# Gram matrices ahead of the values, side steps that may be put off, and a start that turns x a quarter at a time

## The chip, the cores and the metric

One core of a Trainium2 chip runs the whole program. Its engines are TensorE (PE, with a weight-load path PEld beside it), VectorE (DVE), ScalarE (ACT), GpSimd (POOL) and SyncE (SP, which here only issues DMAs). The time is the device time of one execution in microseconds; the median of three runs stands for a kernel, and one further run was profiled.

## The reference, cut to what matters

The layer normalizes x (256 x 2048), multiplies it by one large matrix (2048 x 20672) and feeds three branches: A is block attention over 12 heads of 128, B a recurrence (RWKV7) over 24 heads of 64, C attention to a memory over 4 heads of 256. The three are gated, projected, summed, multiplied by w_out and added to x.

```python
h = rms_norm(x, norm_g)
proj = h @ w_in                       # 2048 x 20672
qkv_a, z_a, rkv_b, z_b, lw, la, q_c, z_c, gates = split(proj)
y_a = moba_attention(q_a, k_a, v_a, rel_bias) * silu(z_a)
# branch B: per head a 64x64 state, one step per token
sa    = state @ a_t
state = state * w_t + outer(sa, b_t) + outer(v_t, k_t)
y_t   = state @ r_t
y_b = (groupnorm(y) * lnx_w + lnx_b + bonus) * silu(z_b)
y_c = memory_cross_attention(q_c, mem_n @ w_mem_kv) * silu(z_c)
merged = g_a*(y_a @ w_proj_a) + g_b*(y_b @ w_proj_b) + g_c*(y_c @ w_proj_c)
out = rms_norm(x + merged @ w_out, final_norm_g)
```

The kernel does branch B in chunks of 128 tokens: for each head a Gram matrix of the chunk's vectors, the solution of a triangular system, and a few products with it.

## The kernel before, in words

**The main stream.** All weights come from HBM in chunks of 512 KB (384 KB for the first job, the LoRA inputs lw and la) into a `raw` buffer (three of them; SP issues the DMA). ACT copies a chunk's high half into a `wt` buffer (L270), DVE writes what is left as the low half (L273) and so frees `raw` for the next DMA. PE multiplies the split weights by the split, transposed x (`hT`): L308 with 512 columns needs the high half only, L309 with 256 columns the low half; "wide" jobs use L306. Sums go into four PSUM banks `pm`. A chunk of a job is a round: `prefetch` starts DMAs and splits up to three chunks ahead (in the first four rounds only the chunk of the round itself), `issue_mm` issues the products for two halves f = 0 and 1, and `step_lanes` then runs one step of each side lane. A round of 16 products takes PE about 2.8 us.

**The side lanes** are generators; what one step issues lands on the engines' queues behind that round's products. Each engine works its queue in order, so a side matmul that waits holds up the next round's main products. Side matmuls share four other PSUM banks, `psd`. `pairs_lane(g)`, for the six groups g of four heads of branch B, computes the decays, the scaled r and k (`AR`, `BK`), then in one step, after V has come, turns two products to sum them per head (L590, L591), turns V and part of BK (L599 to L601) and starts `rw_lane(g)`: the Gram matrices of two token chunks c = 0 and 1 on PE (L622), which DVE scales and masks into `GS` (L626, L627), one step each. Blocks of GS go through DRAM (SP, L652 out and L663 back as `NB`), DVE solves the triangular systems (L674, L678), and further products follow. `attn_a(g)` is branch A's attention: scores, softmax, transposed probabilities, product with v. `later` starts a small lane such as `spread_rows`, whose DMA `fr<-fd` (L421, on ACT's queue) copies a row of the attention's bias to 128 rows.

**The start.** `x_stats` sums squares of x, keeps PE busy with transposes of an identity, and splits the first chunk with its low half held back. `x_quarter(q)` scales 512 columns of both token halves (ACT one, DVE the other, L916 and L917) and transposes them (L154); its `fin` moves the transposes into `hT` as a high half (ACT, L159) and a low half (DVE, L162). Round 0 of the LoRA job does quarters 0 and 1; rounds 1 and 2 begin with quarters 2 and 3. At round 3 the parameter rows and the bias table are turned (L118, L413), the bias is sent to DRAM from ACT's queue (L415), and behind that ACT takes the next job's splits.

## Time and profile before

| | us |
| --- | --- |
| runs | 1479.2, 1479.53, 1478.37 |
| median | 1479.2 |
| profiled execution, own time | 1478.29 |
| its span | 1476.5 |
| outside the span | 1.8 |
| PE busy | 1449.2 |
| DVE busy | 946.2 |
| ACT busy | 747.3 |

The profiled execution is 0.9 us below the median, so a difference worked out in its span is carried to the median as it is. PE is the engine to read: what it waits for, and where.

### The profile page before, as it was taken

How to read it: one execution, taken by the hardware profiler on the slowest of the kernel's cores; microseconds unless marked ns; L12 is line 12 of the kernel's file. 1: busy time of each engine (PE TensorE's matmuls, PEld its weight loads, DVE VectorE, ACT ScalarE, POOL GpSimd, SP SyncE). 2: the span in 40 equal slices, each digit the busy share in tenths (PEclk: the TensorE clock that was granted, in tenths of full speed). 3: DMA queues.
4: the chain of work that ended last, by engine and by line, in shares of the span. 5: the costliest groups of instructions: out<-in, count | busy, mean ns of one | idle time of the engine just before them, and what ended most of it. 6: DMA issues, size and time to landing. Idle time of an engine off the chain costs nothing.

```text
span 1476.5 us, 22151 instructions
## 1 busy us (share of the span) xinstructions
PE 1449.2 (98%) x8315; PEld 1222.3 (83%) x8315; DVE 946.2 (64%) x1855; ACT 747.3 (51%) x1122; POOL 181.8 (12%) x252
## 2 busy tenths in 40 slices
PE   7999999999999999999999999999999999999997
PEld 6887888888888788788888888888888888888887
DVE  5778697796795786784666555655545545545555
ACT  5546546466456456445666454643443444444443
POOL 4312202212212222211100000000000000000011
PEclk9999999999999999999999999999999999999999
DMA  5665555456465465465575555566556556555753
GB/s 180 192 179 163 159 147 169 143 167 173 133 184 151 134 172 159 135 178 158 162 221 187 172 169 174 167 196 192 187 188 195 188 187 194 188 188 192 262 200 130
DMA packets 207968, 258.88 MB, mean 175 GB/s; under 512 B 28172, under 2 KB 146596, under 8 KB 207220
## 3 DMA queue, kind: packets, MB, share of 16 engines
q1 hardware_dynamic: 201872, 247.11, 54.5%
q10 hardware_dynamic: 4164, 6.71, 1.3%
q0 software_dynamic: 1824, 3.65, 0.8%
q8 instruction: 65, 1.06, 0.3%
q14 instruction: 43, 0.35, 0.1%
HBM read 253.74 MB, written 6.05 MB: 176 GB/s over the span
## 4 chain that ended last, share of the span: by engine, by line
PE 89%; DVE 4%; DMA 2%; ACT 1%; issue 1%; POOL 1%; SPq 0%; ACTq 0%; DVEq 0%
PE pm L306 43%; PE pm L308 24%; PE pm L309 12%; PE psd L622 2%; DVE wt L273 1%; DMA raw<-in_w_in_dram 1%; DVE fs_t L674 1%; PE psd L641 1%; PE psd L1037 1%; PE psd L743 1%; DMA NB<-d 1%; PE psd L154 1%; DMA x_sb<-in_x_dram 1%; ACT wt L270 1%; DVE X L678 1%
## 5 line engine op out<-in xcount | busy, mean ns | idle before, releaser
L273 DVE TENSOR_TENSOR wt<-raw,wt 128x1024 fp32r<-128x1024 f32 (+1 forms) x451 | 559.1, 1242 | 437.4 <-ACT wt L270 433.8
L270 ACT ACTIVATE wt<-raw 128x1024 fp32r<-128x1024 f32 (+1 forms) x452 | 477.2, 1057 | 494.0 <-PE pm L306 256.5
L308 PE MATMUL pm<-hT,wt 128*128 128x512 f32 (+1 forms) x1632 | 587.1, 402 | 0.0
L309 PE MATMUL pm<-hT,wt 128*128 128x256 f32 (+1 forms) x1632 | 458.5, 281 | 3.5 <-DVE wt L273 3.4
L308 PEld LDWEIGHTS pm<-hT,wt 128*128 128x128 f32 (+1 forms) x1632 | 305.7, 187 | 76.3 <-issue 4.2
L306 PE MATMUL pm<-wt,hT 128*128 128x512 f32 x1440 | 335.4, 391 | 0.0
L306 PEld LDWEIGHTS pm<-wt,hT 128*128 128x128 f32 x1440 | 268.6, 188 | 57.6 <-issue 1.7
L309 PEld LDWEIGHTS pm<-hT,wt 128*128 128x128 f32 (+1 forms) x1632 | 307.5, 188 | 6.2 <-DVE wt L273 6.0
L306 PE MATMUL pm<-wt,mg 128*128 128x512 f32 (+1 forms) x384 | 79.3, 367 | 0.0
L306 PEld LDWEIGHTS pm<-wt,mg 128*128 128x128 f32 x384 | 65.7, 189 | 12.5
L1183 POOL MEMSET sso<- 128x16 f32 x1 | 0.1, 117 | 607.0 <-PE pm L306 607.0
L674 DVE TENSOR_TENSOR fs_t<-X,NB 128x30 f32<-128x30 f32 (+13 forms) x354 | 64.9, 223 | 7.5 <-DMA NB<-d 7.1
L306 PE MATMUL pm<-wt,yas 128*128 128x512 f32 x288 | 67.6, 395 | 0.0
L306 PE MATMUL pm<-wt,ybs 128*128 128x512 f32 x288 | 67.6, 395 | 0.0
L323 POOL TENSOR_TENSOR lraw<-lraw,et 128x256 f32<-128x256 f32 (+1 forms) x38 | 45.1, 1207 | 167.2 <-ACT lraw L322 167.2
L306 PEld LDWEIGHTS pm<-wt,ybs 128*128 128x128 f32 x288 | 54.3, 188 | 12.6
L306 PEld LDWEIGHTS pm<-wt,yas 128*128 128x128 f32 x288 | 54.3, 188 | 12.7
L317 ACT ACTIVATE et<-pm 128x256 f32<-128x256 f32 (+1 forms) x112 | 42.6, 382 | 40.3 <-PE pm L309 37.6
L678 DVE TENSOR_TENSOR X<-X,fs_t 128x30 f32<-128x30 f32 (+13 forms) x354 | 56.3, 194 | 0.6
L306 PE MATMUL pm<-wt,mT 128*128 128x512 f32 x192 | 45.8, 395 | 0.0
L308 PE MATMUL pm<-mT,wt 128*128 128x512 f32 x128 | 45.4, 395 | 0.0
L306 PE MATMUL pm<-wt,ycs 128*128 128x512 f32 x192 | 45.3, 395 | 0.0
(299 smaller groups left out, 1324.3 us busy)
## 6 DMA issues: line engine op xcount, KB each, us to landing
raw<-in_w_in_dram SPq DMA_DIRECT2D x320, 512.0 KB, 3.7
raw<-in_w_mem_kv_dram SPq DMA_DIRECT2D x32, 512.0 KB, 3.5
raw<-in_w_out_dram SPq DMA_DIRECT2D x32, 512.0 KB, 4.4
raw<-in_w_proj_a_dram SPq DMA_DIRECT2D x24, 512.0 KB, 4.2
raw<-in_w_proj_b_dram SPq DMA_DIRECT2D x24, 512.0 KB
raw<-in_w_proj_c_dram SPq DMA_DIRECT2D x16, 512.0 KB, 4.4
NB<-d SPq DMA_DIRECT2D x24, 128.0 KB, 3.4
fr<-fd ACTq DMA_DIRECT2D x6, 385.0 KB
```

What stands on the lines that cost most here:

```text
L154: pe.transpose(pv[:, a, t], src[:, t, (k + a) * 128:(k + a + 1) * 128], ident)
L270: act.activation(w[:, :, 0], r, AF.Copy)
L273: eng.tensor_tensor(w[:, :, 1], r, w[:, :, 0].bitcast(FT), OP.subtract)
L306: pe.matmul(ps[:, 0:j.n], l, r, start=first and n == 0, stop=last and n == 2)
L308: pe.matmul(ps[0:j.m], hi, both, start=first, stop=last, skip_group_check=True)
L309: pe.matmul(ps[0:j.m, 256:512], lo, top, start=False, stop=last, skip_group_check=True)
L317: act.activation(t, ps[0:j.m, 256:512], AF.Copy)
L323: pool.tensor_tensor(j.dst[f], j.dst[f], t, OP.add)
L622: pe.matmul(pv[h][:, w].rearrange("p x t -> p (x t)"), BK[rows, q, c, w * 128:(w + 1) * 128], AR[rows, q, c].rearrange("p x t -> p (x t)") ...
L641: pe.matmul(pv[:, 2 * q + h], GS[:, c * 4 + 2 * q + h, 2], tok[:, q, c, rows], start=(c == 0), stop=True, skip_group_check=True)
L674: dve.tensor_tensor(t, X[:, k0:8, c:c + 1].to_broadcast([128, m, hi - lo]), NB[:, lo:hi, c].rearrange("p (o n) -> p o n", o=1).to_broadcas ...
L678: dve.tensor_tensor(X[:, k0:8, lo:hi], X[:, k0:8, lo:hi], t, OP.add)
```

## The change

Four edits. (1) `step_lanes` knows a yield (d, more): after d rounds the step may be put off for up to `more` rounds, until a round in which another lane took a `psd` bank; it stands ahead of the decay products (from g = 1 on), the values, the attention's scores, its transposed probabilities and its product with v. (2) In `pairs_lane` the two summed products no longer wait for V; `rw_lane` is started right behind them, two rounds later it issues the Gram matrices, and the turning of V and BK is a later step of its own. Two waits on `rkv_free` are added, one before the next group's BK is written and one before the solved blocks are copied. (3) `x_quarter` becomes `x_scale` and `x_turn`: before round 0 one quarter is turned (each pair of its transposes in a bank of its own) and another scaled on DVE alone; then, in the middle of rounds 0 to 2 between the two halves f, the next quarter is turned, the one behind it scaled and the turned one moved to `hT`. (4) The first chunk's low half goes to POOL at once in place of DVE later, and the identity transposes before the first real ones are 20 in place of 18.

```diff
@@ -145,21 +148,22 @@
         dve.scalar_tensor_tensor(r, s, 1.5, r, op0=OP.add, op1=OP.mult)
         return r
-    def turned(src, g_nm, dst, k):
-        p = ps_side()
-        pv = p.rearrange("p (a t c) -> p a t c", a=2, t=2)
+    def turned(src, g_nm, dst, k, apart=False):
+        banks = [ps_side()]
+        banks.append(ps_side() if apart else banks[0])
+        pv = [two(p)[:, a] for a, p in enumerate(banks)]
         for a in range(2):
             for t in range(2):
-                pe.transpose(pv[:, a, t], src[:, t, (k + a) * 128:(k + a + 1) * 128], ident)
+                pe.transpose(pv[a][:, t * 128:t * 128 + 128], src[:, t, (k + a) * 128:(k + a + 1) * 128], ident)
         def fin():
             for a in range(2):
                 g = pcol(g_nm, k + a)
-                act.activation(dst[:, k + a, 0], two(p)[:, a], AF.Copy, scale=g)
+                act.activation(dst[:, k + a, 0], pv[a], AF.Copy, scale=g)
             for a in range(2):
                 g = pcol(g_nm, k + a)
-                dve.scalar_tensor_tensor(dst[:, k + a, 1], two(p)[:, a], g, dst[:, k + a, 0].bitcast(FT),
+                dve.scalar_tensor_tensor(dst[:, k + a, 1], pv[a], g, dst[:, k + a, 0].bitcast(FT),
                                          op0=OP.mult, op1=OP.subtract)
         return fin
...
@@ -207,16 +213,26 @@
             yield 1
         add_lane(g(), rest)
+    def step(ln):
+        try:
+            d = next(ln[1])
+            d, more = d if isinstance(d, tuple) else (d or 1, 0)
+            ln[0], ln[2] = clock[0] + d, more
+        except StopIteration:
+            lanes.remove(ln)
     def step_lanes():
         clock[0] += 1
-        for ln in list(lanes):
-            if ln[0] > clock[0]:
-                continue
-            try:
-                d = next(ln[1])
-                ln[0] = clock[0] + (d or 1)
-            except StopIteration:
-                lanes.remove(ln)
+        n = used[0]
+        due = [ln for ln in lanes if ln[0] <= clock[0]]
+        for ln in due:
+            if not ln[2]:
+                step(ln)
+        for ln in due:
+            if ln[2] and ln[0] <= clock[0]:
+                if used[0] != n or clock[0] >= ln[0] + ln[2]:
+                    ln[2] = 0
+                    step(ln)
     def force(*keys):
         n = 0
...
@@ -355,6 +371,8 @@
             if c == 0:
                 j.ps[f] = ps_main()
             products(j, j.ps[f], f, c, w)
+            if f == 0 and j.mid:
+                j.mid(c)
             if end:
                 if j.mode == "wide":
                     j.evac(j.ps[f], f)
...
@@ -514,7 +532,7 @@
         wa = rw.tile([96, 256], FT, name="wa")
         pool.dma_start(wd, w_decay2[0][:, c0:c0 + 256])
         pool.dma_start(wa, w_aaa2[0][:, c0:c0 + 256])
-        yield 3
+        yield (3, 2) if g else 3
         p = ps_side()
         sg = rw.tile([128, 2, 256], FT, name="sg")
         for q in range(2):
...
@@ -572,15 +590,13 @@
         dve.tensor_tensor(AR[:, :, :, 0], c2(kk), ep[:, :, :, 0:128], OP.mult)
         dve.scalar_tensor_tensor(av, av, 1.0, kk, op0=OP.add, op1=OP.mult)
         if g:
-            yield from wait(("gram", g - 1))
+            yield from wait(("gram", g - 1), ("rkv_free", g - 1))
         yield 1
         BK = rw.tile([128, 2, 2, 256], FT, name="BK")
         dve.tensor_tensor(BK[:, :, :, 0:128], c2(av), en[:, :, :, 1:129], OP.mult)
         dve.tensor_tensor(BK[:, :, :, 128:256], c2(km), en[:, :, :, 1:129], OP.mult)
         dve.tensor_tensor(esc, ep[:, :, 0, 128], en[:, :, 1, 0], OP.mult)
         flags["decay_free", g] = True
-        yield 1
-        yield from wait(("V", g))
         yield 1
         for t, o in ((sq, nb), (r, bs)):
             p = ps_side()
...
@@ -591,6 +607,10 @@
             dve.tensor_reduce(o.rearrange("p c q h -> p (c q h)"), p.rearrange("p (u v) -> p u v", u=8), AX.X, OP.add)
         dve.tensor_scalar(nb, nb, 1e-24, -2.0, op0=OP.max, op1=OP.mult)
         dve.reciprocal(nb, nb)
+        add_lane(rw_lane(g, AR, BK, tok, nb, bs, esc), 2)
+        yield 1
+        yield from wait(("V", g))
+        yield (1, 2)
         v = St.pop(("V", g))
         for q in range(2):
             p = ps_side()
...
@@ -604,7 +624,6 @@
                 dve.tensor_scalar(tok[:, q, 3, 64 * h:64 * h + 64], pv[:, 3, 64 * h:64 * h + 64],
                                   nb[:, 0, q, h:h + 1], None, op0=OP.mult)
         flags["rkv_free", g] = True
-        add_lane(rw_lane(g, AR, BK, tok, nb, bs, esc))
         yield 1
     def rw_lane(g, AR, BK, tok, nb, bs, esc):
...
@@ -687,6 +706,7 @@
             nc.sync.dma_start(XN[s], d2[8 * d:8 * d + 8].rearrange("u k r c -> (k r) u c"))
         yield 3
         dve.transpose(XT, XN)
+        yield from wait(("rkv_free", g))
         yield 1
         for s in D4:
...
@@ -832,6 +852,7 @@
         yield from wait(("qa", g), ("ka", g))
         if g:
             yield from wait(("soft", g - 1))
+        yield (1, 2)
         q, k = St[("qa", g)], St[("ka", g)]
         p1_, p0_ = ps_side(), ps_side()
         for h in range(2):
...
@@ -868,8 +889,8 @@
                 pe.transpose(p[:, i * 128:i * 128 + 128], s[:, h, o:o + 128], ident)
             act.activation(pT[:, h], p[:, 0:384], AF.Copy)
         flags["soft", g] = True
-        yield 1
         yield from wait(("va", g))
+        yield (1, 2)
         v = St[("va", g)]
         p = ps_side()
         for h in range(2):
...
@@ -898,36 +917,39 @@
                                      accum_out=sp[:, 1, h:h + 1])
             issue_dma(nc.scalar)
         p = ps_side()
-        pe.transpose(p[:, 0:128], x_sb[:, 0, 0:128], ident)
-        for i in range(18):
-            if i == 11:
+        for h in range(2):
+            pe.transpose(p[:, 0:128], x_sb[:, 0, h * D // 2:h * D // 2 + 128], ident)
+            for i in range(10):
+                pe.transpose(p[:, 0:128], ident, ident)
+            if h == 0:
                 turn_params(prow1, "1", 16)
-            pe.transpose(p[:, 0:128], ident, ident)
         ss = stat.tile([128, 2], FT, name="x_ss")
         dve.tensor_reduce(ss, sp, AX.X, OP.add)
         v, s = rsqrt_a(ss, 2, 1.0 / D, 0, "n")
         issue_dma(nc.scalar)
-        issue_split(hold=held)
+        issue_split(pool)
         norm_r.append(rsqrt_b(v, s, 2, "n"))
-    def x_quarter(q):
+    def x_scale(q, first=act):
         r, cs = norm_r[0], slice(512 * q, 512 * q + 512)
-        act.activation(x_sb[:, 0, cs], x_sb[:, 0, cs], AF.Copy, scale=r[:, 0:1])
+        if first is act:
+            act.activation(x_sb[:, 0, cs], x_sb[:, 0, cs], AF.Copy, scale=r[:, 0:1])
+        else:
+            dve.tensor_scalar(x_sb[:, 0, cs], x_sb[:, 0, cs], r[:, 0:1], None, op0=OP.mult)
         dve.tensor_scalar(x_sb[:, 1, cs], x_sb[:, 1, cs], r[:, 1:2], None, op0=OP.mult)
-        fins[q] = [turned(x_sb, "g", hT, 4 * q + 2 * a) for a in range(2)]
+    def x_turn(q):
+        return [turned(x_sb, "g", hT, 4 * q + 2 * a, apart=(q == 0)) for a in range(2)]
     def lora_pre(c):
         if c == 0:
             x_stats()
-            x_quarter(0)
-            x_quarter(1)
-            held.pop()()
-        elif c < 3:
-            x_quarter(c + 1)
-        for f in fins.pop(c):
-            f()
-        if c == 0:
+            x_scale(0)
+            fins = x_turn(0)
+            x_scale(1, dve)
+            for f in fins:
+                f()
             issue_split(pool)
             consts.append(consts_lane())
             next(consts[0])
...
@@ -935,7 +957,16 @@
             next(consts[0])
             prefetch(3, 6)
-    jobs = [Job(w_in2, LW, 192, 16, hT, lora_evac, m=96, pre=lora_pre, add=pool)]
+    def lora_mid(c):
+        if c < 3:
+            fins = x_turn(c + 1)
+            if c < 2:
+                x_scale(c + 2)
+            for f in fins:
+                f()
+    jobs = [Job(w_in2, LW, 192, 16, hT, lora_evac, m=96, pre=lora_pre, mid=lora_mid, add=pool)]
     RJ, AJ = [], []
     for g in range(NG):
         c = g * 256
```

On PE, in the mains around group g = 1 of branch B, the side work of that group stood like this before (L780 turns the output of the group ahead, L590 the two summed products, L599 to L601 V and BK of one of two head pairs, L622 is the Gram of chunk c; L306 are main products):

```order
L306 MATMUL pm<-wt,hT 128x512 x24
L780 MATMUL psd<-ident,YT 128x128 x4
L590 MATMUL psd<-ident,sg 128x128 x4
L590 MATMUL psd<-ident,R 128x128 x4
L599 MATMUL psd<-ident,V 128x128 x2
L600 MATMUL psd<-ident,BK 128x128
L601 MATMUL psd<-ident,BK 128x128
...
L306 MATMUL pm<-wt,hT 128x512 x12
L622 MATMUL psd<-AR,BK 128x256 x8
```

The same place in the changed kernel (L800 is the old L780, L606 the old L590, L619 to L621 the old L599 to L601, L641 the old L622, L322 the old L306):

```order
L606 MATMUL psd<-ident,sg 128x128 x4
L606 MATMUL psd<-ident,R 128x128 x4
L322 MATMUL pm<-wt,hT 128x512 x12
L800 MATMUL psd<-ident,YT 128x128 x4
L322 MATMUL pm<-wt,hT 128x512 x12
L641 MATMUL psd<-AR,BK 128x256 x8
L619 MATMUL psd<-ident,V 128x128 x2
L620 MATMUL psd<-ident,BK 128x128
L621 MATMUL psd<-ident,BK 128x128
...
L322 MATMUL pm<-wt,hT 128x512 x12
L641 MATMUL psd<-AR,BK 128x256 x8
```

One interruption with 20 transposes has become two, of eight and of four, each a round apart; the eight that turn V and BK now follow the Gram of c = 0 in its interruption. The number of interruptions is the same.

On SP's queue, from the program's first weight load to the triangular system of g = 0 (`d` is the block of GS in DRAM), before:

```order
L259 DMA raw<-in_w_in_dram 128x4x192
L259 DMA raw<-in_w_in_dram 128x4x256 x24
L652 DMA d_951<-GS 32x8x32 x4
L259 DMA raw<-in_w_in_dram 128x4x256
L663 DMA NB<-d_951 32x1024 x4
```

And changed:

```order
L275 DMA raw<-in_w_in_dram 128x4x192
L275 DMA raw<-in_w_in_dram 128x4x256 x23
L671 DMA d_933<-GS 32x8x32 x4
L275 DMA raw<-in_w_in_dram 128x4x256
L682 DMA NB<-d_933 32x1024 x4
```

The Gram's way through DRAM starts one weight load, that is one round, earlier.

On ACT, from the first split to the DMA that takes the bias to DRAM, before (L270 is a split's high half, L916 a scaling of x, L159 four high halves of `hT`):

```order
L270 ACTIVATE wt<-raw 128x4x192
L916 ACTIVATE x_sb<-x_sb,rs_rn 128x512 x2
L159 ACTIVATE hT<-psd,par_138 128x256 x4
L270 ACTIVATE wt<-raw 128x4x192
L916 ACTIVATE x_sb<-x_sb,rs_rn 128x512
L159 ACTIVATE hT<-psd,par_138 128x256 x4
L270 ACTIVATE wt<-raw 128x4x192
L916 ACTIVATE x_sb<-x_sb,rs_rn 128x512
L159 ACTIVATE hT<-psd,par_138 128x256 x4
L270 ACTIVATE wt<-raw 128x4x192
L159 ACTIVATE hT<-psd,par_138 128x256 x4
L415 DMA fd<-fb 12x385
```

And changed (L286, L937 and L163 in their places):

```order
L286 ACTIVATE wt<-raw 128x4x192
L937 ACTIVATE x_sb<-x_sb,rs_rn 128x512
L163 ACTIVATE hT<-psd,par_137 128x256 x4
L286 ACTIVATE wt<-raw 128x4x192
L937 ACTIVATE x_sb<-x_sb,rs_rn 128x512
L163 ACTIVATE hT<-psd,par_137 128x256 x4
L937 ACTIVATE x_sb<-x_sb,rs_rn 128x512
L163 ACTIVATE hT<-psd,par_137 128x256 x4
L286 ACTIVATE wt<-raw 128x4x192
L163 ACTIVATE hT<-psd,par_137 128x256 x4
L286 ACTIVATE wt<-raw 128x4x192
L433 DMA fd<-fb 12x385
```

The third and the fourth split have changed places with the four high halves of `hT` ahead of which they stood; one scaling has gone to DVE.

## Rows read from the trace of the kernel before

**Rows 1.** Waits of PE, then of PEld: us in total, times, longest.
```profile
PE psd L599 <- DVE Y L790: 3.4, 5, 0.9
PE psd L622 <- DVE GS L627: 2.3, 4, 0.6
PE psd L700 <- ACT pT L869: 0.4, 1, 0.4
...
PEld pm L309 <- DVE wt L273: 6.0, 8, 1.2
```
**Rows 2.** Timeline of the start: start, us, engine, line, operation [idle before <- releaser].
```profile
12.41 0.88 DVE L917 TENSOR_SCALAR x_sb<-x_sb,rs_rn 128x512 f32<-128x512 f32 x2
...
13.24 3.54 PE L154 MATMUL psd<-ident,x_sb 128*128 128x128 f32 x16 [3.03 <-ACT x_sb L916]
...
16.54 0.47 PE L308 MATMUL pm<-hT,wt 128*96 128x512 f32 x1
...
16.91 1.85 POOL L273 TENSOR_TENSOR wt<-raw,wt 128x768 fp32r<-128x768 f32 x1 [5.30 <-ACT wt L270]
16.92 2.12 DVE L917 TENSOR_SCALAR x_sb<-x_sb,rs_rn 128x512 f32<-128x512 f32 x1
...
19.43 1.03 PE L154 MATMUL psd<-ident,x_sb 128*128 128x128 f32 x8
...
20.11 1.59 ACT L159 ACTIVATE hT<-psd,par 128x256 fp32r<-128x256 f32 x4
...
21.53 0.90 ACT L270 ACTIVATE wt<-raw 128x768 fp32r<-128x768 f32 x1
...
23.38 0.94 DVE L273 TENSOR_TENSOR wt<-raw,wt 128x768 fp32r<-128x768 f32 x1
...
27.08 0.29 DVE L120 COPY par<-psd 128x128 f32<-128x128 f32 x1 [0.82 <-PE psd L118]
...
31.20 0.39 PE L309 MATMUL pm<-hT,wt 128*128 128x256 f32 x1 [0.44 <-DVE wt L273]
```
**Rows 3.** Timeline, PE and DVE, group g = 1: values, then the first Gram.
```profile
181.61 0.60 PE L780 MATMUL psd<-ident,YT 128*128 128x128 f32 x4
...
184.40 2.98 PE L306 MATMUL pm<-wt,hT 128*128 128x512 f32 x12
187.31 2.00 PE L622 MATMUL psd<-AR,BK 64*128 64x256 f32 x16
188.48 0.48 DVE L626 SCALAR_TENSOR_TENSOR GS<-psd,nb,msk 128x256 f32<-128x256 f32 x1 [1.00 <-PE psd L622]
...
189.21 0.47 DVE L626 SCALAR_TENSOR_TENSOR GS<-psd,nb,msk 128x256 f32<-128x256 f32 x1
189.24 0.98 PE L306 MATMUL pm<-wt,hT 128*128 128x512 f32 x3
```
**Rows 4.** Timeline, PE, group g = 4: values, then the first Gram.
```profile
492.74 0.60 PE L780 MATMUL psd<-ident,YT 128*128 128x128 f32 x4
...
496.07 0.48 PE L308 MATMUL pm<-hT,wt 128*128 128x512 f32 x1
...
499.02 1.56 PE L622 MATMUL psd<-AR,BK 64*128 64x256 f32 x10
...
502.18 0.50 PE L308 MATMUL pm<-hT,wt 128*128 128x512 f32 x1
```
**Rows 5.** Timeline, group g = 0: first Gram, then the triangular system's loads and start.
```profile
80.42 2.78 PE L622 MATMUL psd<-AR,BK 64*128 64x256 f32 x16
...
96.00 1.71 SPq L663 DMA_DIRECT2D NB<-d  x4
...
96.80 0.61 ACTq L421 DMA_DIRECT2D fr<-fd  x1
...
103.18 0.28 DVE L674 TENSOR_TENSOR fs_t<-X,NB 128x16 f32<-128x16 f32 x2 [3.60 <-DMA NB<-d]
```
**Rows 6.** The page, DMA issues: operation and count, size, median us to landing.
```profile
NB<-d SPq DMA_DIRECT2D x24, 128.0 KB, 3.4
```

More of the change, by code (lines that the diff above doesn't have):

```diff
@@ L54, in ps_main @@
         return psum.tile([128, 512], FT, name="pm", bufs=4)
+    used = [0]
     def ps_side():
+        used[0] += 1
         return psum.tile([128, 512], FT, name="psd", bufs=4)
@@ L201, in add_lane @@
     def add_lane(gen, rest=0):
-        lanes.append([clock[0] + rest, gen])
+        lanes.append([clock[0] + rest, gen, 0])
     def later(rest, fn, *a):
@@ L240, in tile_hybrid, with __init__ @@
     class Job:
-        def __init__(self, w, c0, n, kt, a, evac, mode="fm", m=128, before=None, pre=None, add=dve):
+        def __init__(self, w, c0, n, kt, a, evac, mode="fm", m=128, before=None, pre=None, mid=None, add=dve):
             self.w, self.c0, self.n, self.kt, self.a = w, c0, n, kt, a
-            self.evac, self.mode, self.m, self.before, self.pre, self.add = evac, mode, m, before, pre, add
+            self.evac, self.mode, self.m, self.before, self.pre, self.mid, self.add = evac, mode, m, before, pre, mid, add
             self.kc = 2 if mode == "wide" else KC
@@ L861, in attn_a @@
                 act.activation(s[:, h, sl], s[:, h, sl], AF.Copy, scale=sm[:, i, h:h + 1])
-        yield 3
+        yield (2, 2)
         pT = rw.tile([128, 2, 384], FT, name="pT")
@@ L885, in tile_hybrid @@
     norm_r = []
-    fins = {}
     consts = []
-    held = []
     def x_stats():
```

## The prediction

> **What bounds the kernel now.** PE is busy 1449.2 of 1476.5 us, so a change that keeps its matmuls can only win or lose idle time of PE, some 27 us of which the start takes the most. I first read the view of waits by engine, to see what PE stands still for, then the timeline at three places where these waits lie. In the waits [rows 1] the reader is to see three families: side matmuls that wait for DVE to empty a `psd` bank (L599 3.4 us, L622 2.3 us), main products that wait for a low half (PEld L309, 6.0 us in 8 waits) and one wait of the attention (L700, 0.4 us). The timeline of the start [rows 2] shows when the first main product runs (16.54) and when the second job gets its first low half (31.20). Those of g = 1 and g = 4 [rows 3, 4] show what an interruption costs above its matmuls. That of g = 0 [rows 5] shows why low halves come late there. DMA is not the bound: the weights are ahead at all places below.
>
> **The start, +2.8 us.** Before, PE turned two quarters, 16 transposes in 3.54, ahead of its first main at 16.54. Now it turns one, 8 transposes in about 1.8, so that they end near 15.0. The first L308 can go then, but the first L309 needs the first chunk's low half, now on POOL. DVE scales three pieces from 12.41 on, 0.44 each, to 13.73; I let POOL begin there and take its 1.85, to 15.6. Half a round is (19.43 - 16.54) / 2 = 1.45, so half f = 0 ends near 16.8, eight transposes (0.9) and f = 1 follow, and round 0 ends at 19.1 in place of 19.43 [rows 2]. That is all that is won.
>
> From there on a loop is closed that was open before. The split of round i is issued after the middle step of round i - 1, and on ACT it stands behind the four high halves of the quarter turned there, as the order of ACT shows. From the first transpose of a quarter it is 0.68 to ACT's first high half (19.43 to 20.11), 1.59 for four, 0.90 for the split's high half, 0.94 for its low half on DVE: 4.1 us [rows 2]. Round 1's half f = 0 ends at 20.55, so the low half of chunk 2 comes at 24.65. PE would want it after 0.9 of transposes, 1.45 of f = 1 and one L308 of 0.35, at 23.2, and stands 1.4. Half f = 0 of round 2 then ends at 25.75, and the low half of chunk 3 comes at 29.85 (the one before ended at 24.32, that of 23.38). DVE's copy of the parameter rows, 27.08 before, stands behind that low half on DVE's queue, so it starts at 29.9. From that copy to the first low half of the next job it took 31.20 - 27.08 = 4.12 (three small DVE steps, the bias's DMA on ACT's queue, a split), and all of it is in the same order as before: 34.0 in place of 31.20 [rows 2]. PE has ended round 3 at about 32.8, so the low half decides: **+2.8**. If each of the two handoffs is 0.2 faster it is +2.4. If POOL or DVE is held up at the first step, all later steps shift with it: up to +4.1, with 1.3 for the two that lie side by side at 16.91 (2.12 where 0.44 is the work, so 1.7, less 0.3 of round 0 that is slack). What follows hides nothing of it, since PE has no idle time that it does not itself lose.
>
> On the step to POOL a rule of the Trainium skill speaks against the change ("SBUF — State Buffer", section "SBUF: two separate sides"): DVE and GpSimd share a pair of ports, whichever starts first holds it for its whole instruction, and the other is blocked altogether. The trace agrees: beside POOL's 1.85 at 16.91 a DVE scaling that takes 0.44 took 2.12 [rows 2]. By that rule it matters which of the two is first at 12.4 to 12.9; the consequence for the time is a rival below, worked out from the same two rows.
>
> **Gram and values, -3.4 us.** Main and side matmuls are the same in number, and the order of PE shows as many interruptions as before; I count nothing for merging. What changes is who waits for which bank. A transpose takes 0.11 (eight in 1.03 with the last one's tail) [rows 2], so the 20 transposes of the old interruption are 2.2. At g = 1 it took 184.40 - 181.61 = 2.79, 0.6 above that [rows 3]; at g = 4, where the attention holds a bank, 3.33, 1.1 above [rows 4]. The waits of L599, 3.4 us in 5 [rows 1], are the same loss: three groups at 0.6 and two at 1.1 to 1.2 are 4.0 with the tails. These interruptions, of 4 and of 8 transposes, now have banks to spare and wait for nothing. The values' eight transposes go behind the Gram. The Gram alone takes 189.24 - 187.31 = 1.93; DVE starts on its first tile 1.17 after its start and needs 0.73 a tile (188.48 to 189.21) [rows 3]. So the first tile's bank is free at 2.0 and the second's at 2.7; PE is there at 1.93, turns four in 0.44, and waits 0.05 + 0.3 = 0.35. At g = 4 and 5 the Gram has three banks and waits for the first: 502.18 - 499.02 - 1.93 = 1.23 [rows 4], which stays, and behind it the values' banks are free in time. At g = 0 the Gram now costs 2.78 against 2.00 [rows 3, 5], since DVE still has the end of the values' step to do when it comes; with the reductions two rounds ahead and the values behind it, that goes. The sum: g = 0 0.78 - 0.35, g = 1 to 3 three times 0.6 - 0.35, g = 4 and 5 twice 1.1: 0.4 + 0.8 + 2.2 = **-3.4**. If the values wait for nothing it is -4.8; if DVE comes one tile (0.73) late at all six, +1.0.
>
> The new waits on `rkv_free` cost nothing that I can find: they are waits of the program's lanes for a step already issued, and delay the writing of the next BK by rounds in which its Gram isn't due.
>
> **The system of g = 0, -3.0 us.** SP issues NB at 96.00 for 1.71 us and, while that runs, ACT's queue issues `fr<-fd` at 96.80. DVE gets its first operand at 103.18 after 3.60 of idleness [rows 5], 7.2 after the issue; the page's median from issue to landing is 3.4 [rows 6]. DVE, which has both the system and the low halves in its queue, is then late for the next 25 us: of the PEld waits of 6.0, 0.8 belong to 31.20 and 1.2 (the longest) to the round at 58, and about 4 are left for this place [rows 1]. In the changed order SP's blocks go out one weight load earlier (23 in place of 24), one round or 2.8, so NB is issued at about 93, is there at 93 + 1.7 + 3.4 = 98.1, and DVE can start 4 to 5 us earlier: the 3.60 of idleness are gone. The DMA `fr<-fd`, which is not moved, still delays the weights behind it. I take three quarters of the 4: **-3.0**; the ends are -3.6 (all of DVE's idleness) and 0 (the weights, not NB, are late).
>
> **Attention's steps, -0.4 us.** Put off to a round with another interruption, L700's wait of 0.4 for its probabilities [rows 1] goes, as the step has more rounds behind it. If a step that is put off meets full banks instead, I take the longest wait of L599, 0.9, as a loss.
>
> **The sum.** +2.8 - 3.4 - 3.0 - 0.4 = -4.0. The profiled execution took 1478.29, so the same one would take 1474.3; the median of the runs is 0.9 above it, and the forecast is **1475.2**.
>
> **Rivals.**
> - The window stays late (weights behind `fr<-fd` decide, not NB): the third term is 0 and the time 1478.2. For it speaks that the weights share the DMA engines with a transfer that isn't moved; against it that DVE's 3.60 is put down to NB [rows 5].
> - POOL is first at the shared place: DVE's second and third scalings wait from 12.85 for POOL's 1.85 to 14.7 and end at 15.6; the first low half of `hT` follows at 15.6 and takes 0.44, so the first main goes at 16.05 and half f = 0 ends at 17.5 in place of 16.8. All of the start shifts by 0.7: 1475.9. For it speaks the row at 16.92, where POOL was first by 0.01; against it DVE's head start at 12.41, with POOL's input ready only at 12.56. This is where the skill's rule would lead.
> - Slower: DVE meets the Gram late. The Gram is a round earlier and its interruption longer, and a low half (0.94 x 4/3 = 1.25 for a full chunk) may stand ahead of the first tile. DVE had 1.00 of idleness there [rows 3]; two low halves, 2.5, would make the first tile 1.5 late, and PE's main stream stands for it in each of six groups: +9.0, together +5.0, 1484.2. It decides from (3.0 + 4.0) / 6 = 1.2 us late on. Against it speaks that idleness; for it, that the splits of up to three chunks ahead come when ACT gives them.
> - A better end: values that wait for nothing (-4.8), all of the 3.6 and a start of +2.4: -6.2, or 1473.0.
>
> **How the numbers follow.** The forecast has 0.47 with a range of its own of 1473.5 to 1477.0, the window that stays late 0.22, POOL first 0.12, slower 0.10, the better end 0.09. The range of 8 in 10 leaves out the slower case and the far ends: 1471.9 to 1480.0. A measurement of this kernel can tell 0.2%, 3.0 us, from no change: faster is below 1476.2, slower above 1482.2. Three quarters of the forecast's chance, 0.6 of POOL's and the better end give 0.35 + 0.07 + 0.09, with rounding 0.52; slower is its rival's 0.10 and 0.01 for what I don't see; the rest, 0.37, is no change.
>
> **What would show it.** The first L309 near 15.7 and round 0's end at 19.1; the second job's first low half at 34.0, with idle PE ahead of the products of rounds 2 and 3 in the waits of L325; no waits of the L619 transposes beyond 0.4 at g = 0 to 3; the solve of g = 0 starting within 6 us of NB's issue and the waits for low halves between 97 and 131 us gone. I am wrong if the second job's low half comes before 32, or if the first tile of the Gram is late.

## The result, and the profile after

The changed kernel took 1501.75 us (median of 5 runs, 1494.29 to 1502.68), the kernel before 1479.53 in the same comparison: a ratio of 1.0145, 95% interval 1.0122 to 1.0169, so 1.5% slower. The forecast was 1475.2 with a range of 1471.9 to 1480.0. The profiled execution has a span of 1500.9, 24.4 more than before.

These are PE's waits in the changed kernel, then those of its weight loads (us in total, times, longest); they answer to [rows 1].

```profile
PE pm L325 <- DVE wt L289: 7.2, 11, 1.4
...
PE psd L720 <- DMA XN<-d: 4.2, 3, 3.7
PE psd L539 <- ACT Z L723: 3.3, 1, 3.3
PE psd L641 <- DVE GS L646: 2.3, 4, 0.6
PE psd L545 <- ACT Z L723: 2.2, 1, 2.2
PE psd L619 <- DVE GS L646: 1.6, 1, 1.6
...
PEld pm L325 <- DVE wt L289: 12.8, 18, 1.7
```

The waits of the V turnings for `Y` (3.4) are gone, as forecast. In their place stand waits that the kernel before did not have: for XN, the solved blocks that come back from DRAM (3.7 of it at g = 5), and for ACT's copy `Z` (L723) by L539 at g = 0 and L545 at g = 3, the next group's decay products. The main products' waits for low halves have doubled, from 6.0 to 12.8 in PEld's view.

Both programs issue the same 6368 main products in the same order, so the place of the loss can be read by how late the n-th of them starts. The table is worked out from the starts in the traces, in us against the kernel before; the columns after the first are runs told of below.

```
main product n, its place           changed  Gram alone  start alone  put-off alone
  72  second job                      4.7       0.3          5.2           0.6
 568  ahead of XN, g = 0              2.8      -0.9          5.3          -0.4
 592  behind it                      10.6       1.2          5.4           0.3
1424  ahead of XN, g = 2             11.3       0.3          5.3           0.1
1456  behind it                      13.4       3.2          5.2           0.1
1840  ahead of XN, g = 3             14.6       1.2          5.2          -0.1
1872  behind it                      21.7       9.2          5.2          -0.1
2728  ahead of XN, g = 5             17.3      10.8          5.6           0.2
2768  behind it                      24.9      14.9          6.6           5.3
6367  the last                       24.3      14.6          6.3           4.9
```

The loss comes in steps, at the interruption in which L720 (L700 before) uses XN. Of each step in the first two columns 1.3 to 1.6 is no loss: the system's next products (L733, L735) stand a round earlier there and so between the two rows. What is left is large at g = 0, 3 and 5, and small at g = 2, where the changed kernel has no wait. This is the interruption of g = 3 in the changed kernel, in the timelines of PE, ACT and SP.

```profile
461.74 1.09 PE L720 MATMUL psd<-XN,GS 32*32 32x32 f32 x32
462.76 1.10 PE L660 MATMUL psd<-tok,GS 128*128 128x64 f32 x8
463.70 1.08 PE L539 MATMUL psd<-lw_t,wd 96*128 96x256 f32 x4
467.03 2.07 PE L545 MATMUL psd<-la_t,wa 96*128 96x256 f32 x4 [2.24 <-ACT Z L723]
```

```profile
464.04 1.06 ACT L286 ACTIVATE wt<-raw 128x1024 fp32r<-128x1024 f32 x1 [2.57 <-DMA raw<-in_w_in_dram]
...
466.21 0.76 ACT L723 ACTIVATE Z<-psd 32x256 f32<-32x256 f32 x2
```

```profile
453.71 2.52 SPq L701 DMA_DIRECT2D d<-X  x4
456.33 0.55 SPq L275 DMA_DIRECT2D raw<-in_w_in_dram  x1
457.68 1.83 SPq L706 DMA_DIRECT2D XN<-d  x4
459.56 3.56 SPq L275 DMA_DIRECT2D raw<-in_w_in_dram  x3
```

Read them from below. Between 453.71 and 459.56 SP issues the system's DMAs and one chunk of weights, so ACT waits 2.57 for a chunk and begins its split at 464.04. The split and the four copies that end a job (465.00 to 466.19) stand ahead of ACT's copy of Z, which empties L720's bank only at 466.21 and after. The interruption takes four side banks (L720, L660, L539, L545), attention holds one more from its product with v at 457.5 to 534.8, and so L545 gets its bank from Z. PE's stall is paid twice: the matmuls behind it run at half the clock (0.63 and 0.41 us from 469.54 to 473.38, where they take 0.40 and 0.28 otherwise), as the granted clock shows in these stretches (columns: the stretch, its us, then the busy time of PE, PEld, DVE, ACT and POOL with their instructions, the granted clock, the DMA share and GB/s). The 0.50 of the last row is the lower of its two levels, 1.2 GHz.

```profile
461.00:464.00 3.00, 3.00 (x47) 2.64 (x47) 1.58 (x2) 0.47 (x1) 0.00 (x0) 1.00 1.03 326
464.00:468.00 4.00, 1.76 (x6) 1.20 (x5) 1.23 (x1) 3.85 (x10) 2.20 (x3) 0.82 0.57 169
468.00:471.00 3.00, 3.00 (x10) 2.49 (x9) 2.11 (x9) 2.88 (x6) 2.52 (x6) 0.50 0.43 145
```

Before, a like ACT wait was there (3.49 at 447.95), but L521 and L527 were an interruption of their own a round earlier. The one of XN took two banks, those of Z and W, and ACT copied Z as soon as L700 was through:

```profile
447.95 1.06 ACT L270 ACTIVATE wt<-raw 128x1024 fp32r<-128x1024 f32 x1 [3.49 <-DMA raw<-in_w_in_dram]
...
452.73 0.78 ACT L703 ACTIVATE Z<-psd 32x256 f32<-32x256 f32 x2 [0.23 <-PE psd L700]
```

### The profile page after: what moved, and what is told of

Its sections match the earlier page's. It is cut to its first block, busy times and chain, and to the rows that moved or that the text cites. A ratio compares the mean times of both kernels' runs of the same rounds, so it can differ in the third digit from the quotient of the medians.

```text
span 1500.9 us, 22139 instructions
## 1 busy us (share of the span) xinstructions
PE 1459.7 (97%) x8318; PEld 1228.2 (82%) x8318; DVE 941.2 (63%) x1855; ACT 747.5 (50%) x1121; POOL 179.3 (12%) x253
## 4 chain that ended last, share of the span: by engine, by line
PE 76%; DVE 11%; DMA 5%; SPq 2%; issue 2%; ACT 1%; POOL 1%; DVEq 0%; ACTq 0%
PE pm L322 41%; PE pm L324 18%; PE pm L325 9%; DVE wt L289 4%; DVE fs_t L693 3%; DMA raw<-in_w_in_dram 2%; DVE X L697 2%; DMA d<-GS 1%; PE psd L641 1%; DMA NB<-d 1%; PE psd L1068 1%; PE psd L763 1%; ACT wt L286 1%; PE psd L660 1%; SPq L701 1%
## 5 line engine op out<-in xcount | busy, mean ns | idle before, releaser
L286 ACT ACTIVATE wt<-raw 128x1024 fp32r<-128x1024 f32 (+1 forms) x452 | 477.3, 1056 | 506.9 <-PE pm L322 256.0
L322 PE MATMUL pm<-wt,hT 128*128 128x512 f32 x1440 | 335.6, 391 | 0.9 <-DVE wt L289 0.9
L325 PEld LDWEIGHTS pm<-hT,wt 128*128 128x128 f32 (+1 forms) x1632 | 309.5, 190 | 13.2 <-DVE wt L289 12.8
L322 PEld LDWEIGHTS pm<-wt,hT 128*128 128x128 f32 x1440 | 268.5, 188 | 58.3 <-DVE wt L289 1.3
L322 PE MATMUL pm<-wt,mg 128*128 128x512 f32 (+1 forms) x384 | 79.3, 367 | 0.0
L322 PEld LDWEIGHTS pm<-wt,mg 128*128 128x128 f32 x384 | 65.7, 189 | 12.5
L693 DVE TENSOR_TENSOR fs_t<-X,NB 128x30 f32<-128x30 f32 (+13 forms) x354 | 65.3, 224 | 12.5 <-DMA NB<-d 12.1
L322 PE MATMUL pm<-wt,yas 128*128 128x512 f32 x288 | 67.6, 395 | 0.0
L322 PE MATMUL pm<-wt,ybs 128*128 128x512 f32 x288 | 67.6, 395 | 0.0
L322 PEld LDWEIGHTS pm<-wt,yas 128*128 128x128 f32 x288 | 54.3, 188 | 12.6
L322 PEld LDWEIGHTS pm<-wt,ybs 128*128 128x128 f32 x288 | 54.3, 188 | 12.7
L322 PE MATMUL pm<-wt,mT 128*128 128x512 f32 x192 | 45.8, 395 | 0.0
L322 PE MATMUL pm<-wt,ycs 128*128 128x512 f32 x192 | 45.3, 395 | 0.0
```

Of the source, the lines that this page charges most:

```text
L286: act.activation(w[:, :, 0], r, AF.Copy)
L322: pe.matmul(ps[:, 0:j.n], l, r, start=first and n == 0, stop=last and n == 2)
L325: pe.matmul(ps[0:j.m, 256:512], lo, top, start=False, stop=last, skip_group_check=True)
L693: dve.tensor_tensor(t, X[:, k0:8, c:c + 1].to_broadcast([128, m, hi - lo]), NB[:, lo:hi, c].rearrange("p (o n) -> p o n", o=1).to_broadcas ...
```

## The experiments

Theory 1, from the trace above: the loss is made where XN comes back, and the start costs only what it shows by the second job. Its rival: the longer start puts DMAs and splits out of step for the whole run. Each median stands beside that of the kernel before, measured with it.

**The parts alone.** The diff was applied in part: the start (the hunks of `turned`, `Job`, `mid` and the start), the Gram ahead of the values without any put-off, the put-off yields without the rest, and all but the start.

```diff
-        yield from wait(("V", g))
...
+        add_lane(rw_lane(g, AR, BK, tok, nb, bs, esc), 2)
+        yield 1
+        yield from wait(("V", g))
+        yield 1
```

> The kernel before with the start alone changed (a quarter of x turned at a time, the middle steps, the first low half on POOL). Theory 1 (the loss is made at the interruptions where the solved blocks come back, and the start costs only what the trace of the changed kernel shows by its 280th main product): about +5 us, 1484 to 1485. Rival (the later start puts DMA and splits out of step for the whole run): +12 us or more, over 1491.

> The kernel before with the Gram ahead of the values alone; nothing is put off, the values' step comes a fixed round after V. The order shows that even so the decay products of the next group fall into the interruption that waits for the solved blocks (XN). Theory 1: the Gram's and the values' waits give 2 us back, and these merged interruptions cost 2 to 6 us at some of the six groups: 1481 to 1490. Rival (only the put-off steps do the harm): 1476 to 1478.

> The kernel before with the put-off yields alone, at the decay products and the attention's three steps. Theory 1: the scores fall into the stretch in which DVE solves the system, so low halves come late there, and the decay products fall into the interruption that waits for XN at four groups: +6 to +14 us, 1485 to 1493. Rival (put-off is harmless, the Gram's move does it): 1478 to 1481.

> The changed kernel with the start of the kernel before. Theory 1: all but the start's 5 us stays, 1495 to 1498. Rival (the start puts everything out of step): under 1485.

Against 1480.03: the start alone 1483.92 (ratio 1.0022, 1.0012 to 1.0032), the Gram alone 1494.63 (1.0100, 1.0084 to 1.0116), the put-off alone 1482.81 (1.0018, 1.0009 to 1.0028), all but the start 1500.97 (1.0137, 1.0121 to 1.0153). So the Gram's move alone costs 15 us, and the step that I had thought worth -3.4 and -3.0 is the one that loses. The rival on the start is out. The Gram alone and all but the start lie above their expected ranges, the put-off alone below its own. The waits of the Gram run show why the Gram loses by itself:

```profile
PE psd L702 <- DMA XN<-d: 3.3, 6, 1.3
PE psd L527 <- ACT Z L705: 3.0, 1, 3.0
...
PE psd L521 <- ACT Z L705: 2.3, 1, 2.3
```

The whole system lane has moved a round ahead, the decay products have not, and so they meet at L702 without any put-off.

The put-off alone shows something else: it, too, brings the decay products behind XN, at g = 1 to 4, and yet its column in the table shows nothing lost at g = 2 and 3. At g = 3 its interruption takes the same four banks, with attention's bank held beside them, and nobody waits:

```profile
449.87 1.09 PE L715 MATMUL psd<-XN,GS 32*32 32x32 f32 x32
450.89 1.11 PE L656 MATMUL psd<-tok,GS 128*128 128x64 f32 x8
451.83 1.08 PE L536 MATMUL psd<-lw_t,wd 96*128 96x256 f32 x4
452.75 1.03 PE L542 MATMUL psd<-la_t,wa 96*128 96x256 f32 x4
```
```profile
451.00 0.76 ACT L718 ACTIVATE Z<-psd 32x256 f32<-32x256 f32 x2 [0.16 <-PE psd L715]
```

There XN is used in its old round, and the copies that end a job stand ahead of it on ACT (447.61 to 448.80). So four banks in one interruption are no loss by themselves. They become one when this interruption comes a round earlier, where ACT still has a split and the end of a job ahead of Z.

**Is it the merging, or XN that comes too late for its earlier user?** Theory 2: four banks in one interruption, and ACT late behind a split. Three edits to the run with the Gram alone:

```diff
 pool.dma_start(wa, w_aaa2[0][:, c0:c0 + 256])
-        yield 3
+        yield 2            # decay products a round earlier
...
-        yield 3
+        yield 4            # the user of XN a round later
         dve.transpose(XT, XN)
...
-            nc.sync.dma_start(XN[s], d2
+            pool.dma_start(XN[s], d2      # and d2's writing likewise
```

> The Gram moved ahead of the values, as in the run with that part alone, but the decay products' step two rounds after its loads in place of three: they are again an interruption of their own, one round ahead of the one that waits for the solved blocks (XN). Theory 2 (the loss is the merging: 4 side banks in one interruption, the fourth free only after ACT's copy of Z, and ACT stands in a split for weights that SP issues behind the system's DMAs): 1477 to 1482, no wait of the decay products for L705. Rival (the Gram a round earlier lets PE reach XN before it is there, whatever else shares the interruption): 1488 or more, with waits of L702 for XN over 5 us in total.

> The Gram moved ahead of the values, with the step that uses the solved blocks (XN) a round later, so that it stands to the decay products as in the kernel before, and XN has a round more to come. Theory 2: 1476 to 1480. Rival (XN early): the same, since XN gets its round back; so this run alone does not part them, and the pair with the run before it does. If both stay above 1488, both are wrong.

> The Gram moved ahead of the values, merged interruption and all, but the system's result goes out and comes back on POOL's queue and not on SP's, so that the weights are not issued behind it. Theory 2: ACT's splits no longer wait for weights at that place, the copy of Z comes in time, and most of the 14 us goes: 1479 to 1486. Rival (banks alone, or XN early): over 1490.

Against 1479.61: with the decay products a round earlier 1480.99, with XN's user a round later 1483.42, with the system's DMAs on POOL's queue 1514.57. The first gives back 13.2 of the 14.6 us that the run with the Gram alone took over the kernel before, while XN is still used a round earlier: these 13.2 hang on the merging. But the run does two things at once. It takes two banks out of the interruption, and it puts the decay products, 2 us of PE's work, ahead of XN, which so has longer to come: PE waits 0.9 for it in place of 3.3. The second, in which nothing is merged and XN has its old round, stays 3.8 above the kernel before and so above its expectation. The third missed its purpose and the expectation by far: the waits for Z are gone there, but XN itself comes later by POOL's queue, and PE waits for it.

```profile
PE psd L702 <- DMA XN<-d: 17.8, 9, 4.2
```

It therefore says nothing on weights that are late behind the system's DMAs. That part of the chain is read from the trace, and no run took it away by itself.

The fourth bank was then tested by itself: the merged interruption stays, but the product into W's bank goes a round later.

```diff
-        W = from_v(0)
         yield 1
+        W = from_v(0)
```

> The Gram moved ahead of the values alone, the decay products still in the interruption that waits for XN, but the first product with the values (bank of W) a round later, so that this interruption takes three side banks in place of four; when XN comes, how ACT's queue stands and which rounds are merged stay as they were. Theory 2 (the fourth bank): the wait of the decay products for ACT's copy of Z (3.0 us at g = 3 in the run with four) goes and with it the stretch at half the clock behind it; g = 4, where the probabilities' two banks come on top, keeps its loss: 1485 to 1490 in place of 1494.6. Rival (banks don't matter, XN or the weights are late): 1493 or more.

1488.39 against 1479.78 (1.0066, 1.0051 to 1.0082), that is 6 us less than with four banks. At g = 3, L527 follows L521 without a wait:

```profile
447.77 1.09 PE L702 MATMUL psd<-XN,GS 32*32 32x32 f32 x32
448.79 1.13 PE L521 MATMUL psd<-lw_t,wd 96*128 96x256 f32 x4
449.76 1.03 PE L527 MATMUL psd<-la_t,wa 96*128 96x256 f32 x4
```

So the fourth bank is worth 6 of the 13.2. The other 7.2 are only in part at g = 4, where the probabilities' two banks join (L527 waits 2.1 there for Z), as expected: PE also waits 3.2 in all for XN, at g = 0, 2, 4 and 5, about as much as in the run with four banks (3.3). How the rest divides between these waits and the clock behind them no run shows.

**The whole kernel, mended.** First the merging alone is undone, with theory 2 to tell what is left; then the attention's put-off too. For the second and the runs behind it theory 3 was formed from the trace of the first: the scores, put off, fall from DVE's idle time into the solve, and the blocks `d`, a round earlier, land late behind the bias rows `fr`.

```diff
-        yield (3, 2) if g else 3
+        yield 2 if g else 3
...
-        yield (1, 2)            # ahead of the scores
...
-        yield (2, 2)
+        yield 3                 # ahead of the probabilities
...
+        yield 1
         yield from wait(("va", g))
-        yield (1, 2)            # ahead of the product with v
```

> The changed kernel whole (start, put-off, Gram), with the decay products' step alone two rounds after its loads and not put off, so that it is again ahead of the interruption that waits for XN. Theory 2: most of the 22 us goes; what is left is the start's 3 to 5, the put-off steps' 3 to 5 and XN that comes late at g = 5: 1483 to 1490. Rival (the three parts work against each other in more places): 1494 or more.

> The changed kernel with the decay products' step two rounds after its loads and the attention's steps not put off: what stays of the change is the start and the Gram ahead of the values. Theory 3 (with the Gram a round earlier the put-off scores fall from DVE's idle time ahead of NB into the solve, which costs some 10 us on top of the merging): 1482 to 1486, that is the start's 3 to 4 us. Rival (what is left in the run with the merging alone undone is the start and the Gram working together): 1491 or more.

1494.88 against 1479.78 (1.0103, 1.0089 to 1.0118), then 1487.44 against 1480.10 (1.0054, 1.0037 to 1.0072). The first fell outside its expectation and theory 2 with it as the whole story; the second came out 1.4 above its own. Over the kernel before in its own comparison the changed kernel takes 22.2 more, the first of these 15.1, the second 7.3: the merging has 7.1, the attention's put-off 7.8, and 7.3 are left for the start and the rest. By the intervals each of these differences is known to some 4 us. Alone the put-off had cost 2.8.

By the starts of the main products the put-off loses, between these two runs, some 3 us from XN of g = 0 up to that of g = 2, 5 more up to that of g = 3 and 4 at that of g = 5. The last is also the one place at which the put-off alone loses (0.2 to 5.3 in the table). No decay products follow there. Put off for three rounds, the scores of g = 4 are still due when the program needs their buffers for g = 5. It then forces them (`force` in `keep_evac`), which steps every lane once in the middle of a round. So all other lanes come a round of main products earlier: XN of g = 5 is used ahead of product 2736 in the changed kernel, 2752 with the Gram alone and 2764 before, and PE waits for it in both runs with the put-off, the changed kernel and the put-off alone:

```profile
679.28 1.73 PE L720 MATMUL psd<-XN,GS 32*32 32x32 f32 x32 [3.67 <-DMA XN<-d]
```
```profile
664.22 0.69 PE L715 MATMUL psd<-XN,GS 32*32 32x32 f32 x16 [2.15 <-DMA XN<-d]
```

With the Gram the put-off costs more, for a reason that the changed kernel's timeline at g = 2 shows (SP, ACT's queue, DVE):

```profile
300.27 0.60 ACTq L439 DMA_DIRECT2D fr<-fd  x1
```
```profile
305.37 1.99 SPq L671 DMA_DIRECT2D d<-GS  x4
307.82 0.98 SPq L275 DMA_DIRECT2D raw<-in_w_in_dram  x1
314.87 1.71 SPq L682 DMA_DIRECT2D NB<-d  x4
```
```profile
318.97 0.29 DVE L693 TENSOR_TENSOR fs_t<-X,NB 128x16 f32<-128x16 f32 x2 [3.21 <-DMA NB<-d]
...
320.66 0.68 DVE L866 SCALAR_TENSOR_TENSOR as<-psd,bias 128x512 f32<-128x512 f32 x1
321.26 0.41 DVE L867 SCALAR_TENSOR_TENSOR as<-psd,bias 128x256 f32<-128x256 f32 x1
321.59 1.00 DVE L872 TENSOR_REDUCE amx<-as 128x2 f32<-128x512 f32 x2
```

The Gram's blocks `d`, a round earlier, now go out 5.1 us behind the bias rows `fr`, where it was 12.1 before; they take up to 8.5 us to land in place of 4.0, so NB is issued 9.5 after them and the solve starts no earlier than its round did before, while the user of XN comes a round earlier. DVE stands idle 3.21 ahead of the solve, and the scores' 2.1 us, which lie ahead of the solve where they are not put off (at 295.91 before), have been put off into it. From there the low halves are late: PEld's waits for them are 15.3 in all in the run with the merging alone undone and 7.1 without the put-off.

**A version that beats both.** From the Gram's move alone (the values' step may be put off as in the changed kernel): the decay products a round earlier, with their weights' loads issued in the group ahead; then the bias rows three rounds earlier from g = 1 on; then that at g = 1 and 2 only, and the values of g = 0 three rounds behind the Gram.

```diff
+        if g + 1 < NG:
+            load_wda(g + 1)     # behind decay_free, group g
...
-            later(4, spread_rows, g + 1)
+            later(1 if g in (1, 2) else 4, spread_rows, g + 1)
...
-        yield (1, 2)
+        yield (1, 2) if g else 4
```

> The start and the attention as in the kernel before; the Gram ahead of the values, which follow it in its interruption; the decay products a round earlier, and their loads issued in the group before, so that they are not waited for (3.7 us of waits in the run with the earlier step). Theory 2: 2 to 4 us below the kernel before, 1475.5 to 1478. Rival (XN a round earlier costs as much as the Gram gives back): 1479 to 1482.

> As the run with the Gram ahead, decay products a round earlier and their loads early, and with the bias rows (fr) of the next group sent three rounds earlier from g = 1 on, so that the Gram's blocks (d) no longer go out some 5 us behind them. Theory 3: at g = 2 and 3 NB is issued about 4 us after d in place of 9, the solve starts 4 us earlier there, the time is 1 to 3 us lower than the run before, 1476 to 1478. Rival (the late NB is hidden there anyway): 1478.5 to 1480.5, the same as the kernel before.

> As the run with the Gram ahead, the decay products a round earlier and their loads early (1479.3), with two more steps: the bias rows sent three rounds earlier at g = 1 and 2 alone (there this took 2 us off the stretch of the solves at g = 2 and 3; at g = 4 and 5 it made the scores wait 4 us for POOL), and at g = 0 the values' step three rounds behind the Gram, so that it does not wait behind two low halves of DVE (1.4 us). Theory 3: 2 to 4 us under that run, 1475.5 to 1477.5, and with it under the kernel before. Rival (such waits come back elsewhere, as in all runs so far): 1478.5 to 1480.5.

1479.34 against 1479.78 (1.0000, 0.9991 to 1.0010), 1482.18 against 1480.10 (1.0012, 1.0002 to 1.0022), 1474.47 against 1479.41 (0.9968, 0.9956 to 0.9980). The first came out as its rival had it, level with the kernel before. The second took the collision away (NB 4.9 us behind d at g = 2) and won 2 us there, but at g = 4 and 5 its earlier bias rows made the scores wait 4.1 for POOL, so it missed. The last is the fastest kernel of the study, 5 us under the one before and 1 below its expectation. Its two steps were not run apart; by the starts 3.1 of the 6.1 us between it and the first are won ahead of XN of g = 0, and 1.9 more by XN of g = 3. SP at its g = 2 shows the collision gone.

```profile
294.45 1.99 SPq L676 DMA_DIRECT2D d<-GS  x4
297.74 0.39 SPq L274 DMA_DIRECT2D raw<-in_w_in_dram  x1
299.09 1.71 SPq L687 DMA_DIRECT2D NB<-d  x4
```

**The start.** The start alone once more, with the next split issued right behind the high halves:

```diff
             for f in fins:
                 f()
+            if c < 2:
+                issue_split()
```

> The changed start alone, with the splits of the third and fourth chunk issued a round earlier, right behind the high halves in the middle of rounds 0 and 1. Theory (the start loses by the split that stands behind the high halves of the quarter just turned): the second job's first low half comes near 31 to 32 in place of 35.9, and the time is that of the kernel before, 1478 to 1481. Rival (the start loses by POOL at the shared place and by PE at half its clock in round 0): 1482 to 1484 as with the start alone.

1482.09 against 1479.61 (1.0017, 1.0008 to 1.0027). In its trace the second job's first low half comes at 32.97, 1.8 late in place of 5.2 (36.38 with the start alone), so the split behind the high halves is most of the start's loss by then. The median fell by less, from 3.9 over its own kernel before to 2.5, which is 1.4 us, and the two intervals overlap: it lies where the rival had it, and what POOL and the half speed told of below cost was not run by itself.

## Why the prediction was wrong, point by point

**The step that failed** is the sentence "I count nothing for merging". I counted the interruptions and their matmuls and looked at the values and the Gram, where banks became free, but not at the other side steps that the moved lane would run into. The count was right and hid it: through the six groups both traces have 102 interruptions, but five groups have one more at the values and five one less at XN. The order of the changed kernel has L539 and L545 behind L720 at five of six groups; four banks in one interruption, at g = 3 with a fifth held by attention, was the place to look. Whether it costs anything hangs on where ACT stands then, as the put-off alone shows. It costs 7.1 us in the changed kernel and 13.2 with the Gram's move alone.

**Gram and values, -3.4.** By the starts of the main products around them, the interruptions of this step are 0.3 shorter at g = 1 to 3, 1.0 at g = 4 and 5 and 0.8 longer at g = 0: -2.1. The mechanism was right, the sizes a little high, except at g = 0. There two low halves (2.35) stand on DVE ahead of the first tile, as the slower rival had it, but at that one group; the V turnings wait 1.6 (L619).

**The system of g = 0, -3.0.** NB was to be issued 3 us earlier. Beside the shifted start it was 2 earlier, and DVE still stood idle for it:

```profile
104.48 0.28 DVE L693 TENSOR_TENSOR fs_t<-X,NB 128x16 f32<-128x16 f32 x2 [2.97 <-DMA NB<-d]
```

It was 3.60 in [rows 5]; PE's waits for low halves between 96 and 137 us fell from 2.2 to 1.1. By the starts, from main product 368 to 568 the Gram alone wins 1.9, and the changed kernel as much beside the probabilities, which stand behind 568 there. So the term was right in kind and a third too large at its place: the waits were halved, not gone, and the rival "the window stays late", with nothing for this term, was wrong too. At g = 2 and 3, of which I had said nothing, the earlier blocks met `fr`, and that is a loss the term does not have.

**The start, +2.8.** The chain was the one forecast, and the first low half of the second job came at 35.90 against 31.20 [rows 2], +4.7; as a whole the start costs 3.9 us alone. Two things were not in the sum, the first of them a rival of the prediction. POOL came first at the shared place:

```profile
12.47 1.92 POOL L289 TENSOR_TENSOR wt<-raw,wt 128x768 fp32r<-128x768 f32 x1 [1.04 <-ACT wt L286]
```
```profile
12.63 2.04 DVE L939 TENSOR_SCALAR x_sb<-x_sb,rs_rn 128x512 f32<-128x512 f32 x1
```

A scaling that takes 0.47 (the one behind it, at 14.60) took 2.04, so DVE's head start was no bar: POOL got in between the first scaling and the second. This is the lock that the Trainium skill states ("SBUF — State Buffer", section "SBUF: two separate sides"), and the trace agrees. And half f = 0 of round 0 ran at half speed, after PE had stood still for 1.1 ahead of the turnings:

```profile
16.27 0.63 PE L324 MATMUL pm<-hT,wt 128*96 128x512 f32 x1
16.70 0.41 PE L325 MATMUL pm<-hT,wt 128*96 128x256 f32 x1
```

They took 0.40 and 0.28 in the rounds behind. Before, the slow stretch lay in the 16 transposes, 0.22 each where the eight behind them took 0.13 [rows 2].

**Attention's steps, -0.4.** This is the second step that failed, and its sign was wrong: the put-off costs 2.8 alone and 7.8 in the whole kernel. I had asked what the step would meet on PE, not that its DVE work had a place ahead of the solve, nor that the program forces scores that are still due and so brings XN of g = 5 forward.

**The sum.** Start 3.9 alone, merging 7.1 and put-off 7.8 are 18.8 of the 22.2; the rest no run parts, the late NB at g = 2 and 3 and the V turnings at g = 0 are in it. The parts are not independent: the put-off costs 2.8, 6.3 (all but the start against the Gram alone) or 7.8 depending on what stands beside it, so no split of the sum is the only one. That the three parts run alone add up to 21.3 (3.9, 14.6 and 2.8) is luck. A slip of the prediction's own: its better end adds up to -6.4 and 1472.8, not -6.2 and 1473.0.

## What to carry to other kernels

When a side step is moved, list for every round which other steps it now shares the round with, and count the buffers that they take together against those that are free, with those that a step holds for long; fewer waits at the old place are worth nothing if the new round needs one buffer more than there are, and the engine that empties them has other work ahead in its queue. Work that lies in another engine's idle time has a place although nothing names it: move the step around it and the place is lost. When a step is put off, look for what forces it while it is still due. And ask of each DMA that is moved what was sent shortly ahead of it, on any queue.

## What the runs showed of the hardware

The small writes `d<-GS` (median 3.0 us to land before, 3.4 in the changed kernel) took up to 8.5 us when they went out 5 us behind the 385 KB of `fr`, although another queue had sent those, up to 5.3 when it was 10 us (put-off alone) and up to 4.0 when it was 12 us. After a stall of 3.0 us (g = 3, Gram alone, up to 454.66) the granted clock was 0.50 from 454 to 457; L527 took 2.08 in place of 1.08, and the main products took 0.63 and 0.41 until 460.4, so the stall cost about 1 and 1.5 us again. At the start of the changed kernel the main products from 16.27 to 18.2 show the same half speed while the column of the granted clock says 1.00: there the lengths of the matmuls tell it, not the column.
